# An encoder trunk on one core: its first hundred microseconds reordered, one upper tile pool, embeddings' low parts by DMA

## The chip, the cores and the metric

The kernel runs on one core of a Trainium2 chip. The metric is device time in microseconds of one execution on that core; lower is better. "Before" is the kernel as it stood, "after" is the kernel with the change.

## The reference, cut to what matters

Two layers over 512 positions of width 1024. The change touches mostly the beginning of layer 0: RMSNorm, one input projection whose columns give q, k, v and u, and a bidirectional state-space layer (S5) that works on u.

```python
def rms_norm(x, g):
    y = xf * lax.rsqrt(jnp.mean(xf * xf, axis=-1, keepdims=True) + EPS)
    return y * g

def na_s5_mixer(h, w_in, rpb, ...):
    z = h @ w_in                       # 512x1024 @ 1024x2048
    q, k, v, u = jnp.split(z, 4, axis=-1)
    a_out = neighbourhood_attention(q, k, v, rpb)       # 8 heads x 64
    b_out = s5_glu(s5_bidirectional(u, ...), w_glu, b_glu)   # 32 groups x 16, state 64
    return jnp.concatenate([a_out, b_out], axis=-1) @ w_out

def reference(x, p, ...):
    for i in range(DEPTH):             # 2
        h = rms_norm(x, ...)
        x = x + (na_s5_mixer if i % 2 == 0 else retention_mixer)(h, ...)
        x = x + conv_ffn(rms_norm(x, ffn_norm[i]), ...)     # width 2816, centred conv over 3 positions
        gate = jax.nn.sigmoid(rms_norm(x, ple_norm[i]) @ ple_w_gate[i])
        x = x + gate * (p[i] @ ple_w_proj[i])               # p[i]: 512x256 embeddings
    return rms_norm(x, final_norm)
```

## The kernel before, in words

**Products.** Everything is held transposed: a tile `t` has 128 features on its partitions and 512 positions along it, so the activation x is eight such tiles. Each float32 operand is split in two parts of reduced width, high (a rounded copy, type fp32r) and low (the rest), and a product of one 128-wide block of outputs with eight input tiles is 24 matmuls of 128x512: for each k the low weight with the high x (`L141`), high with high (`L142`), high with low x (`L143`). `proj` makes one such product into one PSUM tile `ps`.

**Weights.** The weights come in 241 chunks of 128x1024; for the first layers a chunk is one product. SyncE's queue (SP) loads them in order into three raw buffers `wr`; a chunk is split three chunks ahead of its product. The high part `wh` is a ScalarE copy (`L113`). The low part `wl` is a VectorE subtract (`L121`, `L123`), but for the chunks in the range `WL_DMA` (6 to 15) ScalarE writes the negated rounded chunk and a GpSimd DMA adds the chunk from memory to it (`L118`, `L119`).

**Beginning of layer 0.** Scale by the norm's weights and split x (`L177` on ScalarE for the high part, `L178` on VectorE for the low one), squares of x for the mean (`L209`), and `prep_small`, a list of small operations on 32-wide tiles for S5 (powers of lambda), of which `do(n)` issues the next n. Then four products for u (`up`); `Rstd` sums the squares over partitions by matmuls with ones (`L241`) and makes 1/rms on VectorE and GpSimd (`v`, `r`); the first product for q (`q0`); `spread` turns 1/rms into a row (`L252`, copied to SBUF by ScalarE in `L255`). `u_out` multiplies u by that row on VectorE, stores it to a scratch in DRAM (`L566`) and loads it back rearranged as `U` (`L567`). `prep_w1` builds S5's input matrices on VectorE (products of `p1r`, `p1i` with 128x512 tiles, line 168), `trans_w1` transposes them (8 matmuls, `L487`, copied by ScalarE in `L489`), and `states` multiplies them with U (`L591`), after every second product. Then follow the other q products, k and v, attention with the S5 recurrence beside it, and the rest of the layer.

**Order of the work.** In this first region the order of ScalarE and VectorE is that in which the code issues (`manual_schedule`); behind it a scheduler places instructions. Each engine executes its instructions strictly in order, and so does SP with the DMAs it issues.

**Tiles.** `T()` takes a 128x512 tile of a pool of 53 buffers (`NT`). With `special=True` it takes one of an extra pool that each feed-forward (20 buffers) and the retention layer (16) opens and closes.

```python
        w_split(3)
        do(99)
        up.append(proj(xg))
        prep_b()
        up.append(proj(xg))
        prep_w1(0, "r")
        up.append(proj(xg))
        prep_w1(0, "i")
        up.append(proj(xg))
        st_ = Rstd(ss, D)
        q0 = proj(xg)
        st_.spread()
        rr, rc = st_.row, st_.col
        for m in range(4):
            u_out(m)
```

Of the kernel before, what the change touches and what calls it, by code (L numbers as in the profile page):

```python
# [53 lines left out]
DO_X = (0, 0, 0, 6, 6, 6, 6, 6)  # L54
# [3 lines left out]
WL_DMA = (6, 16)  # L58
# [3 lines left out]
def trunk_kernel(ctx, tc, xn, xp, pT, wts, vec, s5bc, ddiag, bias, cs, dst, ident, out):  # L62
# [12 lines left out]
    extra = [None]  # L75

    def T(dt=F32, shape=(128, 512), special=False):
        seq[0] += 1
        if special and extra[0] is not None:
            return extra[0].tile(list(shape), dt, name=f"e{seq[0]}", tag="e")  # L80
        return tp.tile(list(shape), dt, name=f"t{seq[0]}", tag="t")
# [63 lines left out]
    def proj(xs):  # L145
        ps = PS()
        for k, x in enumerate(xs):
            mm3(ps, weights(), x, k == 0, k == len(xs) - 1)
        return ps
# [20 lines left out]
    def split(src, scale=None, low=None, special=False):  # L170
        h, l = T(F32R, special=special), T(F32R, special=special)
# [61 lines left out]
    class Rstd:  # L233


        def __init__(self, ss, n):
            ps = PS()
            parts = ss.parts()
# [10 lines left out]
        def spread(self):  # L249
            pr = PS()  # L250
            for j in range(4):
                pe.transpose(out=pr[:, 128 * j:128 * j + 128], in_=self.col[:, j:j + 1].to_broadcast([128, 128]),  # L252
                             identity=idn)
            self.row = T()
            act.activation(out=self.row, in_=pr, func=ACTF.Copy)  # L255
# [4 lines left out]
    class Next:  # L260
# [25 lines left out]
    def mixer0():  # L286
# [15 lines left out]
        svec = sp.tile([128, 96], F32, name="svec")  # L302
        nc.sync.dma_start(out=svec, in_=vec[:, V_LRE:V_LRE + 96])
# [51 lines left out]
        def prep_small():  # L355
# [39 lines left out]
            for have in (1, 2, 4):  # L395
# [11 lines left out]
                q(tt, dve, pwi[:, 1 + have:1 + have + n, :], x, y, ALU.add)  # L407
            lo, hi = slice(0, 64), slice(64, 128)
            for src, a, b in ((pwr, p1r, p2r), (pwi, p1i, p2i)):
                av = a.rearrange("p g j -> p j g")  # L410
                q(act.activation, out=av[lo], in_=src[lo, 7::-1, :], func=ACTF.Copy)
                q(act.activation, out=av[hi], in_=src[hi, 0:8, :], func=ACTF.Copy)
            q(dve.tensor_copy, MA[:, 0, :], pwr[:, 8, :])
# [19 lines left out]
        def prep_blk():  # L433
# [5 lines left out]
            for name in ("r", "i"):  # L439
                for half in range(2):  # L440
                    t = T()
                    v = t.rearrange("p (g d h) -> p g d h", d=2, h=16)
                    pool.memset(t, 0.0)
# [91 lines left out]
        ss = SumSq(dve)  # L535
# [20 lines left out]
        for k in range(KD - SQ_LAG, KD):  # L556
            ss.add(xt[k], sq=True)
# [23 lines left out]
        rr, rc = st_.row, st_.col  # L581
        for m in range(4):
            u_out(m)
        ts(cim, cim, -1.0)
# [91 lines left out]
        for n in range(8):  # L676
            if n < 7:
                prep_w1(n + 1, "r")
                prep_w1(n + 1, "i")
            if n == 2:  # L680
                prep_blk()
            ps = proj(xg) if n else q0
# [7 lines left out]
            if n:  # L690
                after_trans(n - 1)
            next_w2(W2_K[n])
        after_trans(7)
# [4 lines left out]
        def fk_load(i):  # L698
            fk[i] = [T(), T()]
            for k in range(2):  # L700
                nc.sync.dma_start(out=fk[i][k], in_=pT[i, k])

# [9 lines left out]
        for kp in range(4):  # L712
# [10 lines left out]
            if kp == 3:  # L723
                fk[0] = [split(t) for t in fk[0]]
# [107 lines left out]
        def fill(count):  # L832

            for _ in range(min(count, len(fills))):
                i, n = fills.pop(0)
                if i == 0 and n == 4:
                    fk[1] = [split(t) for t in fk[1]]
# [133 lines left out]
        ph.close()  # L971
        nx = Next("ffn0", fast=(1, 3, 5, 6, 7))
        for n in range(KD):
            ps = proj(mix5)
            x = T()
# [5 lines left out]
    def ffn(i, cur, key):  # L981
        ph = ExitStack()
        sp = ph.enter_context(tc.tile_pool(name=f"ff{i}", bufs=1))
        extra[0] = ph.enter_context(tc.tile_pool(name=f"fe{i}", bufs=20))
# [5 lines left out]
        for m in range(KF):  # L990
# [10 lines left out]
            for half in range(2):  # L1001
# [4 lines left out]
                c = T()  # L1006
# [9 lines left out]
            use = m < 10  # L1016
            h, l = T(F32R, special=use), T(F32R, special=use)
# [5 lines left out]
        for n in range(KD):  # L1023
            ps = proj(hid)
            x = T()
# [3 lines left out]
        extra[0] = None  # L1029
# [4 lines left out]
    def ple(i, cur, key):  # L1034
        ph = ExitStack()
        nx = Next(key)
        if key == "fin":
            nx.full = ph.enter_context(tc.tile_pool(name="fin", bufs=1)).tile([128, KD, 512], F32, name="full")
# [15 lines left out]
        def finish(n):  # L1054
            t = sig.pop(n)
            tt(pool if n < PLE_POOL else dve, t, t, prj[n], ALU.mult)
            x = T()
# [26 lines left out]
    def last_out(cur, prj, row, nx, before):  # L1084
# [10 lines left out]
        xl, sq = nx.full[:, KD - 1], T()  # L1095
# [64 lines left out]
    def retention(cur, key):  # L1160
# [3 lines left out]
        extra[0] = ph.enter_context(tc.tile_pool(name="rte", bufs=16))  # L1164
# [15 lines left out]
        def gated(h, sg, ss):  # L1180
# [6 lines left out]
            def two():  # L1187
                hs[0].spread()
                for e in range(4):
                    tt(dve, sg[e], sg[e], hs[0].row, ALU.mult)  # L1190
                    ys[4 * h + e] = split(sg[e], low=pool, special=4 * h + e < 7)
# [66 lines left out]
        extra[0] = None  # L1258
        ph.close()
        nx = Next(key)  # L1260
        for n in range(KD):
# [5 lines left out]
            x = T()  # L1267
# [122 lines left out]
```

## Time and profile before

| | |
|---|---|
| time, median of 3 runs | 1525.79 us (1525.31 to 1527.48) |
| the profiled execution | 1527.03 us, of which 1525.2 us are the span |
| mean granted TensorE clock | 0.991 of full speed |
| TensorE matmul busy | 1495.3 us, 98% of the span |
| VectorE, ScalarE, GpSimd busy | 60%, 40%, 24% |
| share of the chain that ended last | TensorE 84%, VectorE 7% |

The span is the part of the execution that the profile covers; 1.8 us of the profiled execution lie outside it. Busy shares are over the whole span, so a stage with another limit is seen only when the span is cut in stretches. In the rows below PE is TensorE's matmuls, PEld its weight loads, DVE VectorE, ACT ScalarE, POOL GpSimd, SP SyncE.

### The profile page before, as it was taken

To read this page: it belongs to the slowest core of one execution; us is meant where nothing else is said; L and a number is where in the kernel's file an instruction comes from. 1 tells how busy PE (TensorE), PEld (TensorE's weight loads), DVE (VectorE), ACT (ScalarE), POOL (GpSimd) and SP (SyncE) were. 2 spreads that over 40 slices of the span, in tenths; PEclk is the share of its full clock that TensorE was granted. 3 is DMA by queue.
4 is the path that set the end of the run, shared out by engine and by line. 5 is a ranking of instruction groups with operands and counts; after the bars stand their busy time and mean duration, and the time that the engine had idled before them with its cause. 6 is when DMAs were issued, how large, how long until landed. Compare 5 with 4: busy or idle time off the path is not lost.

```text
span 1525.2 us, 18170 instructions
## 1 busy us (share of the span) xinstructions
PE 1495.3 (98%) x7152; PEld 1234.6 (81%) x7152; DVE 915.7 (60%) x1225; ACT 615.1 (40%) x859; POOL 363.9 (24%) x256
## 2 busy tenths in 40 slices
PE   7899999999999999999999999999999999999998
PEld 5687788888888888887888888888888888888887
DVE  8778966877676523485454544534467676743346
ACT  6344755544444322343434232422244444432233
POOL 0100001233232212063141231413122222212105
PEclk9799999999999999999999999999999999999999
DMA  5854392333333433333222222213333333333331
GB/s 198 219 111 141 102 255 61 94 107 97 98 96 98 120 93 93 120 126 108 72 70 84 68 84 69 83 56 97 97 97 97 97 97 97 97 97 96 97 125 56
DMA packets 58934, 158.95 MB, mean 104 GB/s; under 512 B 11744, under 2 KB 15968, under 8 KB 58848
## 3 DMA queue, kind: packets, MB, share of 16 engines
q1 hardware_dynamic: 57408, 152.55, 32.9%
q0 software_dynamic: 1440, 5.24, 2.1%
q8 instruction: 56, 0.92, 0.2%
q14 instruction: 30, 0.25, 0.1%
HBM read 149.94 MB, written 7.83 MB: 103 GB/s over the span
## 4 chain that ended last, share of the span: by engine, by line
PE 84%; DVE 7%; issue 6%; DMA 1%; POOL 1%; ACT 1%; SPq 0%; DVEq 0%; POOLq 0%; ACTq 0%
PE ps L141 27%; PE ps L143 27%; PE ps L142 27%; DVE t L168 4%; PE ps L591 1%; PE ps L926 1%; DMA t<-in_xp_dram 1%; DVE wl L123 1%; DVE t L277 1%; DVE t L774 0%; PE ps L816 0%; PE ps L241 0%; PE ps L487 0%; POOL t L175 0%; DMA vecs<-in_vec_dram 0%
## 5 line engine op out<-in xcount | busy, mean ns | idle before, releaser
L141 PE MATMUL ps<-t,wl 128*128 128x512 f32 x1568 | 615.9, 393 | 11.3 <-DVE wl L551 6.8
L142 PE MATMUL ps<-t,wh 128*128 128x512 f32 x1568 | 611.8, 390 | 0.0
L143 PE MATMUL ps<-t,wh 128*128 128x512 f32 x1568 | 608.8, 390 | 0.7 <-DVE t L277 0.7
L113 ACT ACTIVATE wh<-wr 128x1024 fp32r<-128x1024 f32 x241 | 254.4, 1059 | 556.2 <-PE ps L143 277.5
L123 DVE TENSOR_TENSOR wl<-wr,wh 128x1024 fp32r<-128x1024 f32 x228 | 298.2, 1309 | 288.9 <-ACT wh L113 288.8
L141 PEld LDWEIGHTS ps<-t,wl 128*128 128x128 f32 x1568 | 296.2, 189 | 75.5 <-DVE wl L551 6.8
L143 PEld LDWEIGHTS ps<-t,wh 128*128 128x128 f32 x1568 | 295.8, 189 | 64.2 <-DVE t L277 1.8
L142 PEld LDWEIGHTS ps<-t,wh 128*128 128x128 f32 x1568 | 296.3, 189 | 60.2
L168 POOL TENSOR_TENSOR t<-t,t 128x512 f32<-128x512 f32 x117 | 177.9, 1522 | 457.6 <-ACT t L1014 279.3
L168 DVE TENSOR_TENSOR t<-ps,t 128x512 f32<-128x512 f32 (+1 forms) x86 | 59.3, 698 | 114.8 <-PE ps L143 103.4
L168 DVE TENSOR_TENSOR t<-t,t 128x512 f32<-128x512 f32 (+2 forms) x113 | 96.8, 878 | 27.8 <-ACT t L200 20.7
L168 DVE TENSOR_TENSOR pad<-ps,t 128x512 f32<-128x512 f32 x88 | 60.5, 692 | 82.4 <-PE ps L143 82.4
L1010 DVE SCALAR_TENSOR_TENSOR t<-pad,vecs,t 128x512 f32<-128x512 f32 x88 | 102.3, 1164 | 1.4
L168 POOL TENSOR_TENSOR t<-t 128x512 f32<-128x512 f32 x33 | 50.3, 1527 | 190.0 <-DVE t L168 190.0
L141 PE MATMUL ps<-e,wl 128*128 128x512 f32 x216 | 85.4, 395 | 0.0
L143 PE MATMUL ps<-e,wh 128*128 128x512 f32 x216 | 85.3, 395 | 0.0
L142 PE MATMUL ps<-e,wh 128*128 128x512 f32 x216 | 85.2, 395 | 0.0
L175 POOL TENSOR_TENSOR t<-t,t 128x512 fp32r<-128x512 f32 x41 | 58.6, 1446 | 60.1 <-ACT t L174 51.5
L1011 DVE SCALAR_TENSOR_TENSOR t<-pad,vecs,t 128x512 f32<-128x512 f32 x88 | 70.0, 796 | 2.9
L1008 ACT ACTIVATE t<-pad,vecs 128x512 f32<-128x512 f32 x88 | 70.2, 802 | 3.4 <-DVE pad L168 3.4
L141 PE MATMUL ps<-wh,t 128*128 128x512 f32 x160 | 62.6, 391 | 0.0
L143 PE MATMUL ps<-wl,t 128*128 128x512 f32 x160 | 62.3, 389 | 0.0
(212 smaller groups left out, 1314.1 us busy)
## 6 DMA issues: line engine op xcount, KB each, us to landing
wr<-in_wts_dram SPq DMA_DIRECT2D x241, 512.0 KB, 3.6
wl<-in_wts_dram POOLq DMA_DIRECT2D x10, 512.0 KB, 7.5
pj_scr<-t SPq DMA_DIRECT2D x16, 256.0 KB, 5.1
t<-pj_scr SPq DMA_DIRECT2D x16, 256.0 KB, 4.1
t<-in_xp_dram SPq DMA_DIRECT2D x8, 256.0 KB, 5.3
t<-in_bias_dram SPq DMA_DIRECT2D x8, 256.0 KB, 4.1
Tm<-k_scr SPq DMA_DIRECT2D x8, 256.0 KB, 6.7
t<-in_xn_dram SPq DMA_DIRECT2D x8, 256.0 KB, 6.6
```

The lines of the kernel that those rows point to most:

```text
L113: act.activation(out=h, in_=raw, func=ACTF.Copy)
L123: late.append(lambda: dve.tensor_tensor(out=l, in0=raw, in1=f(h), op=ALU.subtract))
L141: pe.matmul(out=ps, lhsT=lhs[1], rhs=rhs[0], start=start, stop=False)
L142: pe.matmul(out=ps, lhsT=lhs[0], rhs=rhs[0], start=False, stop=False)
L143: pe.matmul(out=ps, lhsT=lhs[0], rhs=rhs[1], start=False, stop=stop)
L168: eng.tensor_tensor(out=out, in0=a, in1=b, op=op)
L175: low.tensor_tensor(out=l, in0=src, in1=f(h), op=ALU.subtract)
L277: self.late.append(lambda: dve.scalar_tensor_tensor(out=l, in0=x, scalar=g, in1=f(h), op0=ALU.mult, op1=ALU.subtract))
L591: pe.matmul(out=pw[:, i, :], lhsT=w1t["ri"[c], g // 4][:, 128 * (g % 4):128 * (g % 4) + 128], rhs=U[:, g, :], start=True, stop=True)
L1008: act.activation(out=c, in_=t[:, 1:513], func=ACTF.Identity, scale=vcol(cw + 44 + j), bias=vcol(V_CB + 44 * i + j))
L1010: dve.scalar_tensor_tensor(out=c, in0=t[:, 0:512], scalar=vcol(cw + j), in1=c, op0=ALU.mult, op1=ALU.add)
L1011: dve.scalar_tensor_tensor(out=c, in0=t[:, 2:514], scalar=vcol(cw + 88 + j), in1=c, op0=ALU.mult, op1=ALU.add)
```

## The change

- The two small loads `svec` and `nvec` are issued by ScalarE's queue ahead of the rest, no longer by SP.
- Beginning: 14 matmuls of a tile of ones with itself (`WARM`), which nothing reads. 12 of S5's small operations go ahead of x's first split and two (the sines, which load another activation table) ahead of the second. All eight splits of x come first, then the second weight chunk, then the rest. The first chunk's three matmuls for each k go high·high, high·low x, low weight·high. The squares are eight ScalarE squares added up by VectorE in one tile after the splits.
- `Rstd` stands after the fourth product as before, but its VectorE part ahead of the S5 input matrices of group 0; the spread stands behind the fifth product as before. Matrices for groups 0 and 1 are made ahead; a group's transposes come one product later, so that two q products (`ready`) stand ahead of them. Four `memset` of GpSimd (in `prep_blk`) become ScalarE copies of ones scaled by zero.
- `WL_DMA` begins at chunk 7, so chunk 6's low part is a VectorE subtract.
- The embeddings p (`fk`, two tiles in each layer) are split by two ScalarE operations and an accumulating GpSimd DMA (`fk_split`), no longer by a VectorE subtract.
- One pool `upper` of 20 buffers lives from the end of the mixer of layer 0 to the end and takes x, the 1/rms row, the convolution's tile `c` and the low parts of the last seven of the 22 feed-forward tiles. The extra pools go, and the last norm's tile `full` becomes eight ordinary tiles.

```diff
-DO_X = (0, 0, 0, 6, 6, 6, 6, 6)
+DO_X = (12, 2, 0, 0, 0, 0, 0, 0)
+WARM = 14
+UPPER = 20
-WL_DMA = (6, 16)
+WL_DMA = (7, 16)
...
-    def mm3(ps, lhs, rhs, start, stop):
+    def mm3(ps, lhs, rhs, start, stop, first=False):
+        if first:
+            pe.matmul(out=ps, lhsT=lhs[0], rhs=rhs[0], start=start, stop=False)
+            pe.matmul(out=ps, lhsT=lhs[0], rhs=rhs[1], start=False, stop=False)
+            pe.matmul(out=ps, lhsT=lhs[1], rhs=rhs[0], start=False, stop=stop)
+            return
...
+        svec = sp.tile([128, 96], F32, name="svec")
+        nc.scalar.dma_start(out=svec, in_=vec[:, V_LRE:V_LRE + 96])
+        nc.scalar.dma_start(out=nvec, in_=vec[:, 0:KD])
...
+        wm = PS()
+        for _ in range(WARM):
+            pe.matmul(out=wm[:, 0:128], lhsT=ones, rhs=ones, start=True, stop=True)
         prep_small()
         for k in range(KD):
+            do(DO_X[k])
             xg.append(split(xt[k], scale=nvec[:, k:k + 1]))
-            do(DO_X[k])
...
-            if k == W1_AT:
-                w_split(1)
-            if k >= SQ_LAG:
-                ss.add(xt[k - SQ_LAG], sq=True)
...
+        w_split(1)
+        do(17)
+        w_split(2)
...
+        for k in range(4):
+            square(k)
...
         w_split(3)
+        for k in range(4, KD):
+            square(k)
         do(99)
         up.append(proj(xg))
+        up.append(proj(xg))
+        while late:
+            late.pop(0)()
+        prep_p1()
         prep_b()
-        up.append(proj(xg))
+        prep_m()
+        do(99)
+        for _ in range(2):
+            up.append(proj(xg))
+        st_ = Rstd(squares, D)
+        ready = [proj(xg)]
         prep_w1(0, "r")
-        up.append(proj(xg))
         prep_w1(0, "i")
-        up.append(proj(xg))
-        st_ = Rstd(ss, D)
-        q0 = proj(xg)
         st_.spread()
+        ready.append(proj(xg))
         rr, rc = st_.row, st_.col
         for m in range(4):
             u_out(m)
+        prep_w1(1, "r")
+        prep_w1(1, "i")
...
         for n in range(8):
-            if n < 7:
-                prep_w1(n + 1, "r")
-                prep_w1(n + 1, "i")
+            if n < 6:
+                prep_w1(n + 2, "r")
+                prep_w1(n + 2, "i")
...
-            ps = proj(xg) if n else q0
+            ps = ready.pop(0) if ready else proj(xg)
...
-            if n:
-                after_trans(n - 1)
+            if n > 1:
+                after_trans(n - 2)
             next_w2(W2_K[n])
+        after_trans(6)
         after_trans(7)
...
+        def fk_split(i):
+            for k in range(2):
+                h_, l_ = T(F32R), T(F32R)
+                act.activation(out=h_, in_=fk[i][k], func=ACTF.Copy)
+                act.activation(out=l_, in_=fk[i][k], func=ACTF.Copy, scale=-1.0)
+                pool.dma_start(out=l_, in_=pT[i, k], accum_op=ALU.add)
...
+        upper[0] = ctx.enter_context(tc.tile_pool(name="upper", bufs=UPPER))
...
-                c = T()
+                c = T(special=True)
...
-            use = m < 10
-            h, l = T(F32R, special=use), T(F32R, special=use)
+            h, l = T(F32R), T(F32R, special=m >= KF - 7)
```

Where the order of the instructions changes. First ScalarE at the very beginning; `t` are x's high parts (from raw tiles and `nvec`), `wh` the first two weight chunks' high parts, `sm_` the small S5 tiles. Before:

```order
L177 ACTIVATE t_151<-t_89,nvec 128x512
L550 ACTIVATE wh_139<-wr_97 128x512
L177 ACTIVATE t_157<-t_90,nvec 128x512
L550 ACTIVATE wh_139<-wr_97 128x512
L209 ACTIVATE t_163<-t_89 128x512
L177 ACTIVATE t_165<-t_91,nvec 128x512
L209 ACTIVATE t_169<-t_90 128x512
L177 ACTIVATE t_172<-t_92,nvec 128x512
L348 ACTIVATE sm_dt<-svec 128x32
```

and now:

```order
L187 ACTIVATE t_178<-t_92,nvec 128x512
L567 ACTIVATE wh_139<-wr_100 128x512
L358 ACT_TABLE_LOAD
L358 ACTIVATE sm_ang<-sm_ang 128x32
L358 ACTIVATE sm_kk<-sm_kk 128x32
L187 ACTIVATE t_186<-t_93,nvec 128x512
L567 ACTIVATE wh_139<-wr_100 128x512
L187 ACTIVATE t_192<-t_94,nvec 128x512
L187 ACTIVATE t_196<-t_95,nvec 128x512
```

The squares have left the space between the splits, and the table load for the sines stands behind the first split instead of the fifth.

Second VectorE around 1/rms (`v`, `r`); `t<-p1r,t` and `t<-p1i,t` are the S5 input matrices, `t<-ps,t` is `u_out`. Before:

```order
L168 TENSOR_TENSOR t_388<-t_388,t_389 128x512
L123 TENSOR_TENSOR wl_359<-wr_252,wh_358 128x1024
L245 TENSOR_SCALAR v_432<-ps_426 128x4
L168 TENSOR_TENSOR v_432<-v_432,r_431 128x4 x2
L230 TENSOR_SCALAR v_432<-v_432 128x4
L168 TENSOR_TENSOR r_431<-r_431,v_432 128x4
L168 TENSOR_TENSOR t_478<-ps_287,t_476 128x512
```

and now:

```order
L125 TENSOR_TENSOR wl_370<-wr_245,wh_369 128x1024
L255 TENSOR_SCALAR v_435<-ps_429 128x4
L240 TENSOR_SCALAR v_435<-v_435 128x4
L178 TENSOR_TENSOR r_434<-r_434,v_435 128x4
L125 TENSOR_TENSOR wl_400<-wr_262,wh_399 128x1024
L178 TENSOR_TENSOR t_475<-p1r,t_350 128x512
L178 TENSOR_TENSOR t_476<-p1i,t_355 128x512
L178 TENSOR_TENSOR t_475<-t_475,t_476 128x512
L178 TENSOR_TENSOR t_480<-p1r,t_355 128x512
L178 TENSOR_TENSOR t_481<-p1i,t_350 128x512
L178 TENSOR_TENSOR t_480<-t_480,t_481 128x512
L178 TENSOR_TENSOR t_524<-ps_294,t_490 128x512
```

Group 0's six matrix operations stood ahead of 1/rms and now stand behind it, with chunk 6's low part (`wl_400`) as a subtract between.

Third TensorE around the first S5 states. Before, the last matmul of the seventh product, group 1's transposes, and `states`:

```order
L143 MATMUL ps_596<-t_233,wh_394 128x512
L487 MATMUL ps_630<-idn,t_496 128x128 x4
L487 MATMUL ps_637<-idn,t_501 128x128 x4
L591 MATMUL ps_644<-U,t_557 128x64 x4
L591 MATMUL ps_644<-U,t_635 128x64 x4
L591 MATMUL ps_655<-U,t_564 128x64 x4
```

and now, from the last matmul of the seventh product, with the first and the last matmul of the eighth:

```order
L150 MATMUL ps_606<-t_213,wh_399 128x512
L502 MATMUL ps_640<-idn,t_475 128x128 x4
L502 MATMUL ps_647<-idn,t_480 128x128 x4
L148 MATMUL ps_664<-t_178,wl_444 128x512
...
L150 MATMUL ps_664<-t_213,wh_443 128x512
L502 MATMUL ps_698<-idn,t_540 128x128 x4
L502 MATMUL ps_705<-idn,t_545 128x128 x4
```

Group 0's transposes come behind the seventh product and group 1's (with `states` behind them) behind the eighth, one product later than before.

## Rows read from the trace of the kernel before

**Rows 1.** Windows: start and end, length; busy us (instructions) of PE, PEld, DVE, ACT, POOL; clock, DMA share, GB/s.

```profile
0.00:20.80 20.80, 12.28 (x32) 8.19 (x33) 13.95 (x37) 15.99 (x28) 0.20 (x4) 0.92 0.86 308
20.80:36.40 15.60, 15.60 (x74) 12.82 (x72) 14.91 (x47) 7.67 (x10) 0.44 (x1) 1.00 0.23 69
36.40:46.00 9.60, 8.10 (x31) 6.45 (x32) 5.31 (x11) 1.90 (x2) 1.65 (x2) 0.82 0.77 218
60.00:77.00 17.00, 13.03 (x50) 11.42 (x51) 13.82 (x28) 6.14 (x12) 0.86 (x1) 0.50 0.80 198
121.00:200.00 79.00, 75.20 (x625) 59.28 (x624) 73.72 (x180) 48.73 (x125) 0.00 (x0) 1.00 0.48 125
300.00:1525.20 1225.20, 1216.10 (x5424) 1004.26 (x5422) 681.93 (x754) 449.65 (x568) 339.84 (x226) 1.00 0.31 93
```

**Rows 2.** Timeline of PE to 39 us: start, duration, instruction, [idle before <- releaser].

```profile
6.79 0.79 PE L141 MATMUL ps<-t,wl 128*128 128x512 f32 x1 [6.79 <-DVE wl L551]
...
20.87 0.39 PE L141 MATMUL ps<-t,wl 128*128 128x512 f32 x1
...
22.23 0.39 PE L141 MATMUL ps<-t,wl 128*128 128x512 f32 x1
...
38.00 0.50 PE L141 MATMUL ps<-t,wl 128*128 128x512 f32 x1 [1.50 <-DVE wl L123]
```

**Rows 3.** Timeline of ACT to 48 us.

```profile
8.55 0.72 ACT L177 ACTIVATE t<-t,nvec 128x512 fp32r<-128x512 f32 x1 [0.44 <-DMA t<-in_xp_dram]
9.18 0.62 ACT L209 ACTIVATE t<-t 128x512 f32<-128x512 f32 x1
...
12.73 1.04 ACT L113 ACTIVATE wh<-wr 128x1024 fp32r<-128x1024 f32 x1
...
14.92 1.28 ACT L348 ACT_TABLE_LOAD   x1
16.22 0.23 ACT L348 ACTIVATE sm_ang<-sm_ang 128x32 f32<-128x32 f32 x1
...
47.91 0.57 ACT L255 ACTIVATE t<-ps 128x512 f32<-128x512 f32 x1
```

**Rows 4.** Timeline of DVE from 25 to 53 us.

```profile
25.61 0.19 DVE L168 TENSOR_TENSOR sm_ta<-pwr 128x32 f32<-128x32 f32 x1
...
30.11 0.26 DVE L348 COPY MA<-pwr 128x32 f32<-128x32 f32 x2
...
36.73 1.22 DVE L123 TENSOR_TENSOR wl<-wr,wh 128x1024 fp32r<-128x1024 f32 x1
...
40.93 0.15 DVE L245 TENSOR_SCALAR v<-ps 128x4 f32<-128x4 f32 x1
...
42.83 0.17 DVE L168 TENSOR_TENSOR r<-r,v 128x4 f32<-128x4 f32 x1
48.51 4.06 DVE L168 TENSOR_TENSOR t<-ps,t 128x512 f32<-128x512 f32 x4 [5.52 <-ACT t L255]
```

**Rows 5.** Timeline of PE from 61 to 81 us.

```profile
61.95 1.11 PE L487 MATMUL ps<-idn,t 128*128 128x128 f32 x4 [4.33 <-DVE t L168]
64.95 1.12 PE L487 MATMUL ps<-idn,t 128*128 128x128 f32 x4 [1.90 <-DVE t L168]
66.20 7.06 PE L591 MATMUL ps<-U,t 128*128 128x64 f32 x32
...
80.42 1.04 PE L487 MATMUL ps<-idn,t 128*128 128x128 f32 x8
```

**Rows 6.** Timeline of SP and its queue: the scratch of u.

```profile
49.62 3.29 SPq L566 DMA_DIRECT2D u_scr<-t  x4
61.90 4.22 SPq L567 DMA_DIRECT2D U<-u_scr  x4
```

**Rows 7.** The page's costliest groups, two of the feed-forward's: count | busy, mean ns | idle before.

```profile
L1010 DVE SCALAR_TENSOR_TENSOR t<-pad,vecs,t 128x512 f32<-128x512 f32 x88 | 102.3, 1164 | 1.4
L1008 ACT ACTIVATE t<-pad,vecs 128x512 f32<-128x512 f32 x88 | 70.2, 802 | 3.4 <-DVE pad L168 3.4
```

More of the change, by code (lines that the diff above doesn't have):

```diff
@@ L74, in trunk_kernel @@
     seq = [0]
-    extra = [None]
+    upper = [None]
     def T(dt=F32, shape=(128, 512), special=False):
         seq[0] += 1
-        if special and extra[0] is not None:
-            return extra[0].tile(list(shape), dt, name=f"e{seq[0]}", tag="e")
+        if special and upper[0] is not None:
+            return upper[0].tile(list(shape), dt, name=f"e{seq[0]}", tag="e")
         return tp.tile(list(shape), dt, name=f"t{seq[0]}", tag="t")
@@ L143, in mm3, with proj @@
         pe.matmul(out=ps, lhsT=lhs[0], rhs=rhs[1], start=False, stop=stop)
-    def proj(xs):
+    def proj(xs, between=None, at=0):
         ps = PS()
         for k, x in enumerate(xs):
-            mm3(ps, weights(), x, k == 0, k == len(xs) - 1)
+            if between and k == at:
+                between()
+            w = weights()
+            mm3(ps, w, x, k == 0, k == len(xs) - 1, first=st["cur"] == 0)
         return ps
@@ L237, in __init__ @@
             ps = PS()
-            parts = ss.parts()
+            parts = ss if isinstance(ss, list) else ss.parts()
             for j in range(4):
@@ L442, in prep_blk @@
                     v = t.rearrange("p (g d h) -> p g d h", d=2, h=16)
-                    pool.memset(t, 0.0)
+                    act.activation(out=t.rearrange("p (a b) -> p a b", b=128),
+                                   in_=ones.rearrange("p (a b) -> p a b", a=1).to_broadcast([128, 4, 128]),
+                                   func=ACTF.Copy, scale=0.0)
                     src = v16(bb[name])
@@ L551, in mixer0, with square @@
                 dve.tensor_tensor(out=l[:, p], in0=raw[:, p], in1=f(h[:, p]), op=ALU.subtract)
-            if k == W1_AT:
-                w_split(1)
-            if k >= SQ_LAG:
-                ss.add(xt[k - SQ_LAG], sq=True)
-        for k in range(KD - SQ_LAG, KD):
-            ss.add(xt[k], sq=True)
+        w_split(1)
+        do(17)
+        w_split(2)
+        squares = []
+        def square(k):
+            t = T()
+            act.activation(out=t, in_=xt[k], func=ACTF.Square)
+            if squares:
+                tt(dve, squares[0], squares[0], t, ALU.add)
+            else:
+                squares.append(t)
+        for k in range(4):
+            square(k)
         up = []
@@ L835, in fill @@
                 i, n = fills.pop(0)
-                if i == 0 and n == 4:
-                    fk[1] = [split(t) for t in fk[1]]
+                if i == 0 and n == 2:
+                    fk_split(1)
                 ps = proj(fk[i])
@@ L1028, in ffn @@
         hid.clear()
-        extra[0] = None
         ph.close()
@@ L1037, in ple @@
         if key == "fin":
-            nx.full = ph.enter_context(tc.tile_pool(name="fin", bufs=1)).tile([128, KD, 512], F32, name="full")
+            nx.full = [T() for _ in range(KD)]
         prj = []
@@ L1190, in two @@
                     tt(dve, sg[e], sg[e], hs[0].row, ALU.mult)
-                    ys[4 * h + e] = split(sg[e], low=pool, special=4 * h + e < 7)
+                    ys[4 * h + e] = split(sg[e], low=pool, special=4 * h + e < 0)
             return one, two
```

34 lines of the change are left out of this document (15 added, 19 removed).

## The prediction

> **What bounds the kernel now.** I read the busy table first: TensorE matmuls fill 98% of the span, so only the other 2% and the stretches at a low clock can be won. The windows then say where these lie. From 300 us to the end the engine is busy 1216.1 of 1225.2 us at full clock [rows 1]: 9.1 us in four fifths of the kernel. The beginning is another matter. The price of work at full clock comes from the timeline: from 20.87 to 22.23 us six matmuls of 128x512, 0.227 us each, so 5.45 us a product of 24; at clock 0.50 twice that [rows 2]. By this price the 32 matmuls up to 20.8 us are 7.3 us of work: 13.5 lost, 6.8 of them ahead of the first matmul. From 36.4 to 46 us 1.5 idle and 8.10 busy at 0.82, another 1.5: 3.0 lost. From 60 to 77 us 4.0 idle and 13.03 at 0.50: 10.5 lost, with 2.3 more of the same wait ahead of 60 us (4.33 ended at 61.95) [rows 1, 2, 5]. Some 29 us in all, and the change reorders just this part. What is waited for there: a low part of the first chunk, another low part at 38.00 (VectorE was busy 14.91 of the 15.60 us before), the S5 matrices of group 1 (4.33 and 1.90), and behind these the states, which multiply with U [rows 1, 2, 5].
>
> The 1/rms row explains the 60s: `r` is done on VectorE at 43.0, but ScalarE copies the row at 47.91, behind four operations on weights; VectorE idles 5.52 us until 48.51, and all S5 matrices stand behind `u_out` [rows 3, 4].
>
> **The change, part by part,** as a walk along TensorE, with the times that rows of before give to each piece.
>
> *First product.* The first matmul waited for VectorE's low half, some 0.6 to 0.7 (half of the 1.22 of a whole chunk [rows 4]). High·high goes first now, so it starts at 6.1. ScalarE then has the table load 1.28 and two sines of 0.14 (7.6), x1 at 0.63 from start to start (8.55 to 9.18), the second half of the chunk 0.5 and six splits at 0.63: 12.6; chunk 1's copy 1.04 to 13.6, VectorE's subtract 1.22 to 14.9 [rows 3, 4]. Product 2 starts there if nothing else is late. Two things can be: x7's landing (x2 was there at 8.55; the five others and chunk 1 are 1.8 MB, 6.0 us at the 308 GB/s of that stretch, so 14.5 at the latest and product 2 at 17.2 [rows 1, 3]), or the clock (21 matmuls at 0.454 from 8.3: 17.8). I take 15.7, near the lower end, since ScalarE waited only 0.44 for x2 although squares and small work gave later tiles more time [rows 3]. The two small loads leave SP, which brings the other loads forward by two issues at most, inside these bounds. The warm-up matmuls run while TensorE waits anyway; what they do to the clock lies within 14.9 to 17.8, and if they ran into the first product they would cost their own time, 14 small matmuls.
>
> One rule speaks against the new place of the table load. In rows 3 it takes 14.92 to 16.20 and the next operation starts at 16.22, so it costs 1.28. The Trainium skill, "ScalarE: Activation LUTs", section "What ACT_TABLE_LOAD costs", counts a drain of 1380 ns to it, 2.66 us a switch. By that, an estimate, x1 to x7 would be 1.4 later and the result below 1.4 us higher, 1516.1; the trace doesn't agree, no gap stands there, and the sum goes by the row.
>
> *Products 2 to 4.* 15.7 + 3 x 5.45 = 32.05, sums of squares 0.9: 32.9, where before they ended at 36.5 (38.00 less 1.50) [rows 2]. Lead 3.6, bounds 1.5 to 4.4. VectorE's work up to chunk 4's low part, from 14.9: 17 small operations 2.5 at 0.15, three low parts 3.4 (1.22 less the 0.09 by which neighbours overlap, as at 9.18), seven adds 4.2, powers 4.5 (25.61 to 30.11), 29.5; with 1.5 of waiting for ScalarE's squares 31.0, before TensorE asks at 32.9 [rows 4]. So the 1.50 wait and the low clock behind it (3.0) go. Little cover, 1.9: if it is gone, they come back.
>
> *1/rms.* The S5 input products (six of 0.6 and four copies, 4.3), 0.4 of small copies and chunk 5's low part 1.1 come ahead of it: 36.8; `v` to `r` took 40.93 to 43.0, so 38.9. Product 5 ends at 38.35, so the spread waits 0.6 and takes 0.4: 39.4. Behind the waiting spread stands product 6, nothing else. Bounds: no wait, or 2 us. ScalarE's copy has no weights ahead of it now. VectorE meanwhile does chunk 6's low part (1.1, new, since that chunk no longer goes by DMA) and six matrices of group 0 (3.9), so `u_out` starts at 44.0 and not 48.51, in place of the 5.52 idle [rows 4].
>
> *To the first states.* Products 6 and 7 to 50.3, group 0's eight transposes 0.9 (1.04 in the row at 80.42, the end overlapped), product 8 to 56.6. VectorE: four `u_out` at 1.0 to 48.0, three operations, then fifteen of 0.6 (which the order puts ahead) and the last sum of group 1: 59.6. Group 1's second transposes thus wait some 2.5 us, against 4.33 and 1.90 before, and end at 60.1 [rows 4, 5]. What is late next is U: from the first store's issue to the states it took 49.62 to 66.20, 16.6 us; 45.1 + 16.6 = 61.7 [rows 5, 6]. Bounds: 60.9, where the transposes' copies allow it (0.8 behind them, as 65.4 to 66.20), and 66.2, no earlier than before. I take 61.7, the same trip, as SP has the same four stores and loads among the same weights. States at full clock take half of 7.06: 65.2. Before, this point (eight products, two groups of transposes, two states) was reached at 80.42 [rows 5]. Lead 15.2.
>
> *Clock.* After 4.33 and 1.90 idle it was 0.50, the 1.2 GHz level, for all of 60 to 77; after 1.50, 0.82 in a window of 9.6 [rows 1]. With 2.5 and 1.6 idle I expect the states at half clock, 3.5 us back; bounds nothing, and 3.5 + 2.0 (nine more matmuls).
>
> *Behind.* Transposes 6 and 7 now follow each other after the last product, so their copies are no longer hidden: twice the 0.8, 1.6 back (0 to 3). The embeddings' four subtracts leave VectorE where it is busy 73.72 of 79 us, 2.4 us; TensorE idles 3.8 there [rows 1]. I take 1.0 won (0 to 2.4). Their two new transfers for each layer go on GpSimd's queue, which is idle there (0.00 busy), and ScalarE, 48.73 of 79 busy, has room for the two operations each.
>
> *Nothing:* the pool `upper`, the tiles of the last norm, ScalarE's copies in place of `memset`. The cover: in a feed-forward two tiles `c` are taken for each two products, 10.9 us, and with x, the row and seven low parts as few as 4 buffers are left, good for two such steps; the work on two tiles is some 2 x (0.80 + 2 x 1.16), 6.2 us [rows 7], and without that cover each of 44 steps would wait for the rest. I price it at nothing, bounds 4 us lost and, from the 9.1 idle, 2 won.
>
> Sum: 15.2 - 3.5 - 1.6 + 1.0 = 11.1 us. The profiled execution, 1525.2 of span and 1.8 around it, would go from 1527.0 to 1515.9; it lies 1.2 above the median of the runs shown, so the median goes from 1525.8 to 1514.7.
>
> **Rivals.** Faster or slower means more than 0.2%, 3.05 us, about what a measurement of this kernel tells from no change.
>
> A, the whole lead is kept: no low clock behind the short waits and U at 60.9. For it: after 1.50 idle only part of the stretch was slow. 15.2 + 0.8 - 1.6 + 1.0 = 15.4, 1510.4 (1508 to 1512).
>
> B, U comes no earlier than before, at 66.2, because its stores and loads share the DMA engines with the same accumulating weight transfers (share 0.80 in 60 to 77 [rows 1]). States at half clock to 73.3, nine slow matmuls 2.0: 75.3, lead 5.1, less 1.6, plus 1.0: 4.5, 1521.3 (1519 to 1522.7).
>
> C, VectorE sets the time from `u_out` to attention's end. Its own lead is 4.5, and the late transposes take 1.6: 2.9, 1522.9, within 0.2%. Against it: it idles 3.2 us even in 60 to 77, where it is waited for, and 543 of the last 1225 [rows 1].
>
> D, slower: U's trip grows. SP executes in order, and the fourth store and the loads stand behind weight loads that wait for raw buffers. The states then end at U + 7.1 with 2.0 of slow matmuls; with the 0.6 behind, no gain is left when U comes at 70.7, a trip of 25.6 in place of 16.6. With twice the trip, 33.2, U is there at 78.3: 7.6 lost, 1533.
>
> **How the numbers follow.** My forecast 0.53 (its own range 1512 to 1518.5), A 0.20, B 0.17, C 0.06, D 0.04. A, B and the forecast are faster: 0.90; C the same: 0.06; D slower: 0.04. The range reaches to A and B with the unknown of the feed-forward: 1507.5 to 1521.5; it leaves out C, D and the outer parts of A and B, under 2 in 10.
>
> **What would show it.** In the changed kernel's profile: the first matmul near 6 us, product 2 near 15.7, no wait at the fifth product, VectorE's first `u_out` near 44 and the idle ahead of it gone; the wait at group 1's transposes near 2.5; the first states near 62, and the clock in the 8 us behind. Behind 200 us all should be as before, shifted by some 11 us. I am wrong if product 2 starts behind 18, if the states come behind 66, if the clock stays at half through two products, or if the feed-forward's blocks wait for tiles `c`.

## The result, and the profile after

The kernel after takes 1507.32 us (median of 4 runs, 1506.71 to 1507.82) against 1526.63 (4 runs, 1525.31 to 1528.38) for before: ratio 0.9873, 95% interval 0.9856 to 0.989. That is 19.3 us less. The forecast was 11.1 us less, 1514.7, and its range ended at 1507.5, just above the measured time. The profiled execution has a span of 1505.9 us against 1525.2, so the trace holds the whole difference.

The windows of the kernel after, cut where the work of [rows 1] now lies (columns as there):

```profile
0.00:17.00 17.00, 14.46 (x58) 11.16 (x59) 11.32 (x34) 13.57 (x23) 0.20 (x4) 1.00 0.91 321
17.00:33.00 16.00, 16.00 (x76) 13.41 (x75) 14.96 (x41) 8.74 (x13) 0.00 (x0) 1.00 0.46 139
33.00:41.00 8.00, 7.54 (x35) 5.94 (x35) 6.66 (x17) 3.45 (x5) 2.01 (x2) 1.00 0.50 163
57.00:65.00 8.00, 4.26 (x24) 3.82 (x22) 7.92 (x18) 3.84 (x8) 0.86 (x1) 0.77 1.13 263
65.00:77.00 12.00, 12.00 (x60) 10.23 (x60) 11.94 (x22) 5.71 (x12) 0.86 (x1) 0.87 0.29 85
```

The stretch at clock 0.50 of [rows 1] has shrunk to 0.77 and 0.87 in 20 us, the one at 0.82 is gone, and VectorE is busy nearly all the time from 38 to 77 us (38.55 of 38.90), where it had idled. The timeline of TensorE after, beside [rows 2, 5]:

```profile
1.06 6.07 PE L560 MATMUL ps<-ones 128*128 128x128 f32 x28 [1.06 <-DVE ones L328]
6.89 0.47 PE L144 MATMUL ps<-t,wh 128*128 128x512 f32 x1
...
15.54 0.50 PE L148 MATMUL ps<-t,wl 128*128 128x512 f32 x1 [0.64 <-DVE wl L123]
...
39.00 0.65 PE L262 MATMUL ps<-idn,r 128*128 128x128 f32 x4 [0.46 <-DVE r L178]
...
59.55 0.66 PE L502 MATMUL ps<-idn,t 128*128 128x128 f32 x4 [2.20 <-DVE t L178]
61.75 3.65 PE L627 MATMUL ps<-U,t 128*128 128x64 f32 x16 [1.54 <-DMA U<-u_scr]
65.16 0.77 PE L148 MATMUL ps<-t,wl 128*128 128x512 f32 x1
65.73 0.63 PE L149 MATMUL ps<-t,wh 128*128 128x512 f32 x1
66.16 0.63 PE L150 MATMUL ps<-t,wh 128*128 128x512 f32 x1
...
68.23 0.39 PE L149 MATMUL ps<-t,wh 128*128 128x512 f32 x1
...
70.98 1.89 PE L627 MATMUL ps<-U,t 128*128 128x64 f32 x16
...
73.94 1.04 PE L502 MATMUL ps<-idn,t 128*128 128x128 f32 x8
```

and of VectorE, beside [rows 4]:

```profile
38.78 0.16 DVE L178 TENSOR_TENSOR r<-r,v 128x4 f32<-128x4 f32 x1
...
43.86 4.08 DVE L178 TENSOR_TENSOR t<-ps,t 128x512 f32<-128x512 f32 x4
...
58.81 0.68 DVE L178 TENSOR_TENSOR t<-t,t 128x512 f32<-128x512 f32 x1
```

Up to the first states the walk of the prediction is met to a few tenths, but for the first matmul: it came at 6.89 instead of 6.1, as the warm-up matmuls ran up to then. Where the rest of the 19.3 comes from is read from instructions that both kernels have: the start in before less the start in after is the lead at that place. In before, the first matmul of attention, the first of the block behind it (`Tm`), and 1/rms of three later norms:

```profile
142.95 1.57 PE L761 MATMUL ps<-t,t 64*128 64x256 f32 x12
...
220.55 0.44 PE L926 MATMUL ps<-Tm,U 128*64 128x128 f32 x4
...
646.18 1.93 POOL L168 TENSOR_TENSOR r<-v,mhalf 128x4 f32<-128x4 f32 x1 [39.35 <-DVE v L245]
...
1115.84 1.93 POOL L168 TENSOR_TENSOR r<-v,mhalf 128x4 f32<-128x4 f32 x1 [30.35 <-DVE v L245]
...
1477.95 1.93 POOL L168 TENSOR_TENSOR r<-v,mhalf 128x4 f32<-128x4 f32 x1 [39.36 <-DVE v L245]
```

and in after:

```profile
130.01 1.57 PE L806 MATMUL ps<-t,t 64*128 64x256 f32 x12
...
206.62 0.44 PE L971 MATMUL ps<-Tm,U 128*64 128x128 f32 x4
...
630.59 1.93 POOL L178 TENSOR_TENSOR r<-v,mhalf 128x4 f32<-128x4 f32 x1 [39.02 <-DVE v L255]
...
1098.52 1.93 POOL L178 TENSOR_TENSOR r<-v,mhalf 128x4 f32<-128x4 f32 x1 [30.00 <-DVE v L255]
...
1458.99 1.93 POOL L178 TENSOR_TENSOR r<-v,mhalf 128x4 f32<-128x4 f32 x1 [39.01 <-DVE v L255]
```

The lead is 12.9 at attention, 13.9 behind it, 15.6 at 646 us of before, 17.3 at 1116, 19.0 at 1478 and 19.3 at the end. So 5.4 us come where the prediction priced everything at nothing. In between, during the 22 blocks of each feed-forward, the lead stays the same; it grows during the products that follow them, and during the retention's output product. TensorE waits for nothing there in either kernel. The page of before had the trace of it, in a view that I read for waits only; groups of TensorE from 500 to 640 us, by form, in before:

```profile
L141 PE MATMUL ps<-t,wl 128*128 128x512 f32 x124 | 48.3, 389 | 0.0
...
L143 PE MATMUL ps<-e,wh 128*128 128x512 f32 x80 | 31.6, 395 | 0.0
```

Matmuls that stream a tile `e` of an extra pool last 395 ns, others 389. From start to start it shows better: in before the 30 matmuls of one run over `e` tiles begin at 527.10, the next over a `t` tile at 534.09, 233 ns each, where `t` tiles have 227:

```profile
527.10 0.40 PE L141 MATMUL ps<-e,wl 128*128 128x512 f32 x1
...
534.09 0.39 PE L141 MATMUL ps<-t,wl 128*128 128x512 f32 x1
```

648 such matmuls (3 x 216) at 6.4 ns are 4.1 us of the 5.4.

### The profile page after: what moved, and what is told of

It reads as the page before. It is cut to its first block, busy times and chain, and to the rows that moved or that the text cites. A ratio compares the mean times of both kernels' runs of the same rounds, so it can differ in the third digit from the quotient of the medians.

```text
span 1505.9 us, 18279 instructions
## 1 busy us (share of the span) xinstructions
PE 1487.4 (99%) x7180; PEld 1234.9 (82%) x7180; DVE 910.3 (60%) x1222; ACT 617.3 (41%) x866; POOL 363.4 (24%) x255
## 4 chain that ended last, share of the span: by engine, by line
PE 86%; DVE 5%; issue 5%; DMA 2%; ACT 1%; POOL 1%; DVEq 0%; SPq 0%; POOLq 0%; ACTq 0%
PE ps L148 27%; PE ps L149 27%; PE ps L150 27%; DVE t L178 2%; PE ps L627 1%; DVE wl L125 1%; PE ps L971 1%; DVE e L178 1%; DMA u_scr<-t 1%; DMA U<-u_scr 1%; PE ps L861 0%; DMA t<-in_xp_dram 0%; PE ps L251 0%; PE ps L502 0%; PE ps L1158 0%
## 5 line engine op out<-in xcount | busy, mean ns | idle before, releaser
L148 PE MATMUL ps<-t,wl 128*128 128x512 f32 (+1 forms) x1776 | 693.7, 391 | 1.8 <-ACT t L885 1.0
L149 PE MATMUL ps<-t,wh 128*128 128x512 f32 (+1 forms) x1776 | 689.9, 389 | 0.0
L150 PE MATMUL ps<-t,wh 128*128 128x512 f32 x1664 | 644.6, 389 | 0.9 <-DVE t L287 0.9
L149 PEld LDWEIGHTS ps<-t,wh 128*128 128x128 f32 x1776 | 334.0, 188 | 67.5
L150 PEld LDWEIGHTS ps<-t,wh 128*128 128x128 f32 x1664 | 312.7, 188 | 66.0 <-DVE t L287 1.3
L178 POOL TENSOR_TENSOR e<-e,e 128x512 f32<-128x512 f32 x44 | 58.7, 1334 | 278.9 <-ACT e L1059 278.9
L178 POOL TENSOR_TENSOR t<-t,t 128x512 f32<-128x512 f32 x49 | 77.3, 1582 | 142.8 <-DVE t L178 128.0
L178 DVE TENSOR_TENSOR pad<-ps,e 128x512 f32<-128x512 f32 x88 | 60.6, 692 | 82.8 <-PE ps L150 82.8
L1055 DVE SCALAR_TENSOR_TENSOR e<-pad,vecs,e 128x512 f32<-128x512 f32 x88 | 101.3, 1153 | 2.3
L1056 DVE SCALAR_TENSOR_TENSOR e<-pad,vecs,e 128x512 f32<-128x512 f32 x88 | 70.0, 796 | 2.9
L1053 ACT ACTIVATE e<-pad,vecs 128x512 f32<-128x512 f32 x88 | 70.2, 803 | 3.3 <-DVE pad L178 3.3
L178 POOL TENSOR_TENSOR t<-e,t 128x512 fp32r<-128x512 f32 x30 | 53.7, 1791 | 35.4 <-ACT t L1062 35.4
```

The costliest lines, as they stand in the source:

```text
L178: eng.tensor_tensor(out=out, in0=a, in1=b, op=op)
L1053: act.activation(out=c, in_=t[:, 1:513], func=ACTF.Identity, scale=vcol(cw + 44 + j), bias=vcol(V_CB + 44 * i + j))
L1055: dve.scalar_tensor_tensor(out=c, in0=t[:, 0:512], scalar=vcol(cw + j), in1=c, op0=ALU.mult, op1=ALU.add)
L1056: dve.scalar_tensor_tensor(out=c, in0=t[:, 2:514], scalar=vcol(cw + 88 + j), in1=c, op0=ALU.mult, op1=ALU.add)
```

## The experiments

**Theories.** S: the place at which a streamed tile starts, against the place of the weight tile, sets the pace of a matmul. All ordinary tiles (2048 bytes a partition) and weight tiles (4096) lie one behind the other, so they start at the same place modulo 256 bytes (the trace shows no addresses; the places are worked out from the order and sizes of the pools). In a feed-forward of before four padded tiles of 514 floats, each rounded up to 2080 bytes, lie ahead of the extra pool: 8320 bytes, which is 128 off; in the retention a tile of 32 bytes makes it 32 off. Rival R: how far up in the partition the tile lies. Rival W: waits for buffers.

**Only the start of the extra pools moved.** The kernel before, plus

```diff
         pads = [sp.tile([128, 514], F32, name=f"pad{j}") for j in range(4)]
+        gap = sp.tile([128, 32], F32, name="gap")
...
         lg = sp.tile([128, 8], F32, name="lg")
+        gap = sp.tile([128, 56], F32, name="gap")
```

> The kernel before, with two unused tiles (128 bytes a partition in each feed-forward, 224 in the retention) that only shift the extra pools' start, so that it stands at the same place modulo 256 bytes as the ordinary tiles and the weight tiles. In before 648 matmuls that stream a tile of an extra pool start 233.5 ns apart on the mean, all others 227. Theory S (where a tile starts decides): these come to 227, 4.2 us less in the profile and some 4 to 5 us less in the time, about 1522. Rival R (how far up in the partition the tile lies decides): still 233.5, time as before, within 2 us. Rival W (the late 5.4 us are waits for buffers that the extra pools cause): no change in the pitch, time as before.

Measured 1522.96 us against 1527.88 for before on that chip, ratio 0.9967 (0.995 to 0.9983), 4.9 us. The same run of 30 matmuls in this kernel:

```profile
524.63 0.39 PE L141 MATMUL ps<-e,wl 128*128 128x512 f32 x1
...
531.43 0.39 PE L141 MATMUL ps<-t,wl 128*128 128x512 f32 x1
```

6.80 us, 227 ns each. An unused tile of 128 bytes takes the slow pace away; the tiles lie higher up than before, so R falls, and W with it, since the buffers are the same. From the first `Tm` to the end of the span this kernel takes 1299.4 us, against 1304.6 in before and 1299.2 in after:

```profile
218.29 0.44 PE L926 MATMUL ps<-Tm,U 128*64 128x128 f32 x4
```

Its span is 1517.7. So behind that place the unused tiles alone give as much as the pools of after.

**All streamed tiles moved.** The kernel after, plus

```diff
+    gap = ctx.enter_context(tc.tile_pool(name="gap", bufs=1)).tile([128, 32], F32, name="gap")
     tp = ctx.enter_context(tc.tile_pool(name="act", bufs=NT))
```

> The kernel after, with one unused tile of 128 bytes a partition ahead of the pool of ordinary tiles, so that all tiles that matmuls stream lie 128 bytes off the weight tiles modulo 256 bytes, as the first feed-forward's extra pool did in before. Theory S: nearly all of the 6,072 matmuls of 128x512 go from 227 to some 233 ns, about 40 us more, 1547. Rival R and rival W: no change, 1505 to 1510. A third way, that only a stream from two pools at different places is slow: no change either, since all streamed tiles stay at one place.

Measured 1539.08 us in a single run, some 31 more than after. 300 us of the first feed-forward, in this kernel and then in after:

```profile
300.00:600.00 300.00, 300.00 (x1288) 241.34 (x1287) 175.27 (x182) 114.74 (x143) 73.68 (x49) 1.00 0.32 97
```

```profile
286.00:586.00 300.00, 300.00 (x1326) 248.39 (x1325) 183.40 (x189) 120.31 (x149) 80.35 (x52) 1.00 0.34 101
```

Both are 100% busy at full clock, and one does 38 matmuls fewer: TensorE's busy share of 100% doesn't show this loss. The 40 us that I expected fell short by 8; 1/rms of the first feed-forward comes only 2.0 later (272.14 against 270.13), so the layers ahead of it, with their waits for VectorE, take little part.

**Weights moved as well.** The same gap ahead of `wraw`, so that weight tiles and streamed tiles move together.

> The kernel after with the same unused tile of 128 bytes, but ahead of the weight tiles too, so that weights and streamed tiles move together. If the distance between the two decides: 227 ns and the time of after, 1507. If the place itself decides: 233 ns and 1539, as when the streamed tiles alone moved.

Measured 1507.8 us in a single run, and the same 1326 matmuls in 300 us as after:

```profile
286.00:586.00 300.00, 300.00 (x1326) 248.57 (x1325) 183.07 (x189) 120.11 (x149) 79.68 (x52) 1.00 0.33 100
```

It is the distance between the two operands that counts, not the place.

**Which distances.** The kernel before with gaps of 48, 16 and 16 floats (first feed-forward, retention, second feed-forward), and with 8, 48 and 160.

> The kernel before with unused tiles that set how far the streamed extra tiles start from the weight tiles, modulo 256 bytes: 64 in the first feed-forward (before 128), 96 in the retention (before 32), 192 in the second feed-forward (before 128). Theory S, any offset but 0 is slow: 231 to 235 ns for all three against 227. Rival: a coarser grid decides, so that 64 and 192 are fast (227) and 96 slow.

> As the run with 64, 96 and 192, with 160 in the first feed-forward, 224 in the retention, and in the second feed-forward 0 modulo 256 but 1024 modulo 2048. Theory S with a period of 256: slow, slow, fast (227). Rival, a period of 2048 as the size of a tile: the third is slow as well.

The mean distance of starts in a run over `e` tiles (21 to 30 matmuls):

| distance modulo 256 bytes | 0 | 32 | 64 | 96 | 128 | 160 | 192 | 224 |
|---|---|---|---|---|---|---|---|---|
| ns from start to start | 226.7 | 233.4 | 229.4 | 234.0 | 233.1 | 234.1 | 233.3 | 233.3 |

The last region of the second kernel, 0 modulo 256 but 1024 modulo 2048, has 226.7, so a period of 2048 falls. One of 512 or 1024 falls too: the extra pool of a feed-forward in the first run with gaps starts 8448 bytes, 256 modulo 512, behind the place where `upper` starts in after (by the order of the pools), and both have 227 ns. So 256 is the period. 64 lies between, below the 231 to 235 that I expected; my rival of a coarser grid is half right there and wrong at 192. The times of the two, one run each, were 1526.52 and 1525.12 us.

**The pools alone, and all but the pools.** The kernel before with the pools of after (its `upper`, `special=True` for x, row and `c`, no extra pools, `full` as a list), and the kernel after with the pools of before:

```diff
-        upper[0] = ctx.enter_context(tc.tile_pool(name="upper", bufs=UPPER))
...
+        upper[0] = ph.enter_context(tc.tile_pool(name=f"fe{i}", bufs=20))
...
-            h, l = T(F32R), T(F32R, special=m >= KF - 7)
+            h, l = T(F32R, special=m < 10), T(F32R, special=m < 10)
```

> The kernel before with only the tile pools of after: the pool of 20 from the end of the first mixer, x, row and the convolution's tile in it, low parts of the last seven of 22. The beginning is that of before. By the leads read from the two traces (13.9 us at the first feed-forward, 19.3 at the end) this part is worth 5.4 us: 1526.6 less 5.4 is 1521.2, whatever its mechanism. My prediction's step (the pools are worth nothing) expects 1526.6 within 1.5.

> The kernel after with the pools of before (an extra pool in each feed-forward and the retention, the last norm's tile in a pool of its own): the beginning, the embeddings' split and chunk 6 alone. By the leads 13.9 us faster than before, 1512.7; with the step that the pools are worth nothing it would be the time of after, 1507.3. The 648 matmuls that stream extra tiles are at 233 ns again.

Measured 1523.14 us, ratio to before 0.9967 (0.9956 to 0.9979), 4.7 less; and 1513.4, ratio 0.991 (0.9895 to 0.9924). By ratio that is 0.37% or 5.6 us more than after. These are the two sides of the 5.4; the beginning with the rest of the change is the other 14 us (1527.88 less 1513.4 is 14.5). Which of the edits at the beginning carry the 14 was tested only for those that follow.

**Parts of the beginning.** The kernel after without the 14 matmuls of ones:

```diff
-WARM = 14
+WARM = 0
...
-        wm = PS()
```

> The kernel after without the 14 matmuls of ones at the start. My prediction put the second product between 14.9 and 17.8 us, the upper end if the first product runs at half clock (0.43 us a matmul): if the warm-up is what lifted the clock, the first product's last matmuls are at 0.43, the second product starts near 17.5 instead of 15.54 and the time is about 2 us longer, 1509.3. Rival: the clock rises by itself as the product begins, or product 2 waits for VectorE anyway: within 0.7 of 1507.3.

Measured 1507.66 us (1505.48 to 1510.25), no difference. Its first products:

```profile
6.08 0.79 PE L144 MATMUL ps<-t,wh 128*128 128x512 f32 x1 [6.08 <-ACT wh L566]
...
10.16 0.63 PE L144 MATMUL ps<-t,wh 128*128 128x512 f32 x1
10.58 0.63 PE L145 MATMUL ps<-t,wh 128*128 128x512 f32 x1
...
12.33 0.40 PE L144 MATMUL ps<-t,wh 128*128 128x512 f32 x1
...
15.40 0.50 PE L148 MATMUL ps<-t,wl 128*128 128x512 f32 x1 [0.15 <-DVE wl L123]
```

Matmuls start 0.43 us apart until 11.9 us here, as where the granted clock reads 0.50, and 0.23 behind it, so the warm-up does lift the clock. (The clock column doesn't show this: its first record in this trace begins at 11.85, and it reads 1.00 for 0 to 17 us.) The first matmul starts at 6.08, 0.8 ahead of after's, as no warm-up matmul stands in its way. But product 2 waits for chunk 1's low part in both (0.64 with the warm-up, 0.15 without), and starts at 15.40 instead of 15.54. My expectation let 21 matmuls run slowly, and it was about ten.

Group 0's matrices ahead of 1/rms again:

```diff
+        prep_w1(0, "r")
+        prep_w1(0, "i")
         st_ = Rstd(squares, D)
         ready = [proj(xg)]
-        prep_w1(0, "r")
-        prep_w1(0, "i")
```

> The kernel after with group 0's six matrix operations ahead of 1/rms again. My walk: the spread then waits some 4.3 us in place of 0.5, but u_out starts where it did (both stand ahead of it), product 8 ends at 60.5, group 1's transposes no longer wait, and the states start near 62.0 in place of 61.75; with a stretch at half clock behind the longer wait some 1 to 2 us in all, 1508.3 to 1509.3. Rival, the earlier 1/rms carries the gain by itself: the whole 4 us, 1511.5.

Measured 1507.82 us (1505.93 to 1508.37), ratio to before 0.9868 (0.9854 to 0.9883). The wait that was put back, and the first states:

```profile
42.85 1.11 PE L262 MATMUL ps<-idn,r 128*128 128x128 f32 x4 [4.27 <-DVE r L178]
...
64.21 1.90 PE L627 MATMUL ps<-U,t 128*128 128x64 f32 x16
```

The rival's 1511.5 falls. The 4.27 us of waiting cost nothing, for behind it the 2.20 and the 1.54 are gone and the states run at full clock (1.90 against 3.65). They start 2.2 later than my walk said, as the half clock now comes behind the 4.27, in product 6, yet the next transposes start at 73.30 against 73.94 in after. TensorE's idle time between 15 and 107 us is 4.9 us here and 4.8 in after: it only changed its place.

Transposes one product later still:

```diff
-            if n > 1:
-                after_trans(n - 2)
+            if n > 2:
+                after_trans(n - 3)
...
+        after_trans(5)
         after_trans(6)
```

> The kernel after with the transposes of a group yet one product later (three q products ahead of the first, the last three groups behind the last product). In after TensorE waits 2.2 us for group 1's transposes and 1.5 for U, and works at half clock for some 3 us behind. If these waits are only a matter of when U and the matrices are ready, a product fills them: the states start near 63 without a wait, and 5 to 6 us are won, 1501.5 to 1502.5. Rival, the time moves on: transposes and states together behind the last product give 1 to 2 us back, 1503 to 1504. Rival, VectorE sets the time from there on: within 1 us of 1507.3.

Measured 1504.0 us (1502.16 to 1507.43), ratio to before 0.9846 (0.9826 to 0.9867): the fastest of all, 0.27% or 4.1 us ahead of after by the ratios, whose intervals overlap a little. This is the upper end of the rival by which the time moves on. A product fills the waits but for 1.24 here and 0.60 ahead of the states at 92.61:

```profile
64.60 2.00 PE L627 MATMUL ps<-U,t 128*128 128x64 f32 x16 [1.24 <-ACT t L504]
...
101.51 0.44 PE L531 MATMUL ps<-t,t 128*128 128x128 f32 x2
```

The last row stands at 106.28 in after, so 4.8 us are won by then, but 1/rms of the first feed-forward comes only 2.7 earlier (267.43 against 270.13): attention gives 2.1 back. Part of that is the clock, at half behind a wait of 1.1 there, where after has 1.00 throughout (columns as in [rows 1]):

```profile
157.00:161.00 4.00, 3.88 (x14) 3.20 (x14) 4.00 (x18) 3.75 (x14) 0.00 (x0) 0.57 0.18 66
```

The embeddings' low parts on VectorE again:

```diff
-                act.activation(out=l_, in_=fk[i][k], func=ACTF.Copy, scale=-1.0)
-                pool.dma_start(out=l_, in_=pT[i, k], accum_op=ALU.add)
+                tt(dve, l_, fk[i][k], f(h_), ALU.subtract)
```

> The kernel after with the embeddings' low parts as VectorE subtracts again (at the same places, without the accumulating transfers). My prediction gave their removal 1.0 us (0 to 2.4), and the lead grows by 1.0 in the attention stage (12.9 at its first matmul, 13.9 behind it): 1508.3 if it is this. Rival: the 1.0 comes from the attention's other waits falling differently, within 0.4 of 1507.3.

Measured 1511.37 us, ratio to before 0.9893 (0.9879 to 0.9908), by ratio 0.20% or 3.1 us more than after. From the last place named to the first `Tm`, its longest wait, and the window behind this wait:

```profile
107.15 0.44 PE L531 MATMUL ps<-t,t 128*128 128x128 f32 x2
...
209.75 0.44 PE L970 MATMUL ps<-Tm,U 128*64 128x128 f32 x4
```

```profile
PE ps L830 <- ACT t L848: 2.6, 1, 2.6
```

```profile
162.00:165.50 3.50, 3.39 (x24) 2.22 (x23) 3.40 (x12) 2.85 (x8) 0.00 (x0) 0.51 0.20 75
```

102.6 us, against 100.34 in after (106.28 to 206.62), 2.3 more, which is about the 2.4 us of four subtracts. Not all of it is waiting: ScalarE, for which TensorE waits 2.6, had waited 1.45 and 0.96 for VectorE, and behind this wait the clock is at half for some 3.4 us, which after doesn't have. 0.9 more were lost ahead of it, where U came at 61.80 with a wait of 1.80; that the edit did this isn't shown, and kernels with the same beginning differ as much there.

## Why the prediction was right and wrong

| step | predicted | measured |
|---|---|---|
| first matmul, product 2 | 6.1, 15.7 | 6.89, 15.54 |
| sums of squares done, r done | 32.9, 38.9 | 32.9, 38.9 |
| u_out, wait of group 1's transposes | 44.0, 2.5 | 43.86, 2.20 |
| first states | 61.7 | 61.75 |
| lead behind them, clock taken off | 15.2 - 3.5 = 11.7 | 11.9 |
| "Behind": up to attention | -1.6 | +1.0 |
| embeddings, net of attention | +1.0 | +1.0 |
| "Nothing": pools and the rest | 0 | +5.4 |

The 11.9 is 80.42 [rows 5] less 73.94 - 5.45, since one more product stands ahead of the third transposes now. These leads come from one pair of traces. The first states start between 64.59 and 67.41 in five kernels with the beginning of before, and between 60.89 and 61.80 in six with the order of after (one of them without the warm-up), so the leads up to there are good to some 1.5 us, and that 61.7 was met to a tenth is in part luck. The 14 us of the whole beginning rest on the medians of the runs above.

**The step that failed** is "*Nothing:* the pool `upper`", priced at 0 where 5.4 us were won. It looked for buffers that come free too late and found cover, rightly: in both feed-forwards the lead doesn't move. That the change of pools also changes where streamed tiles start wasn't in it at all. The bound of 2 us won was drawn from the 9.1 us of idle time, and the gain lay in the busy time, where 648 matmuls took 233 ns each. The run with gaps of 128 and 224 bytes shows that as the cause: from the first `Tm` to the end it takes 1299.4, 5.2 less than before, and the kernels with the pool `upper`, but for the one with all streamed tiles moved, take 1299.2 to 1300.5. The count of matmuls gives 4.1 of the 5.2; the other 1.1 lies within the 1.3 by which these kernels differ. With nothing for the pools the time would have been in the range: the kernel after with the pools of before took 1513.4.

**"Behind" had the wrong sign.** It claimed that transposes 6 and 7 now follow each other, and are no longer hidden. They did so in before, with the copy's wait that I charged to the change:

```profile
113.07 1.91 PE L487 MATMUL ps<-idn,t 128*128 128x128 f32 x16
115.58 2.00 PE L591 MATMUL ps<-U,t 128*128 128x64 f32 x16 [0.60 <-ACT t L489]
```

After has 48 records of states in one piece behind them and no wait. I had read the loop's end as new when it was old.

**The `memset`,** also under "Nothing", were not nothing. In before a VectorE operation beside them takes 2.80 us, and it stands ahead of the matrices of group 1, for which TensorE waited 4.33:

```profile
52.48 2.80 DVE L331 TENSOR_SCALAR t<-t 128x512 f32<-128x512 f32 x1
...
52.75 2.25 POOL L443 MEMSET t<- 128x512 f32 x4
```

In after, with ScalarE's copies, it stands behind these matrices and takes 0.42:

```profile
59.41 0.42 DVE L341 TENSOR_SCALAR t<-t 128x512 f32<-128x512 f32 x1
```

So it is in every trace: 1.49, 1.86, 1.92 and 2.80 us where it overlaps the `memset`, 0.44 in the one kernel where it ends ahead of them (64, 96 and 192 bytes), 0.41 to 0.43 in the eight kernels without them. The walk doesn't name this operation, and what its 2.4 us are worth in the time no run shows.

**The clock term** held for another reason than stated. Only 16 of the 32 records of states ran at half clock, 1.8 us; seven matmuls behind them gave 1.4 more: 3.2 in place of 3.5. The price of half clock was also too high: such a matmul starts 0.43 us behind the last (65.73 and 66.16 above), 1.9 times the 0.227, not twice.

**The embeddings** came out at 1.0 net, which must be 2.3 won and about 1.3 of the lead given back in attention: with the subtracts its stretch up to `Tm` takes 78.87 us, against 77.60 in before. That would be rival C's mechanism on a small scale, and the version with transposes one later shows such a loss directly (2.1 of 4.8), a part of it by the clock. Rivals A, B and D did not come: from the first store's issue at 44.96 to the states at 61.75 it is 16.8 us, against 16.6 in before [rows 5, 6].

**The table load's rule.** By the Trainium skill, "ScalarE: Activation LUTs", section "What ACT_TABLE_LOAD costs", x1's split would have come 1.4 us later, an estimate. The load ran from 6.24 for 1.28 us and the next operation began at 7.53; the trace doesn't agree with the drain, as before. (In before the load stood behind the sixth split of x, not the fifth: that split starts at 14.20, the load at 14.92.)

## What to carry to other kernels

Look at the distance from start to start of equal matmuls, not only at waits and busy shares: a group that is a few per cent slower than its twin is a finding, and moving a pool can change it without any edit of the work. Lay streamed tiles and weight tiles so that they start at the same place modulo 256 bytes (shown here for float32r matmuls of 128x512 alone); an odd tile ahead of a pool undoes it for all behind. And before a wait is priced as a gain, follow what stands behind it: 4.3 us put back at the spread cost nothing here, since as much waiting went away behind it.

## What the hardware showed that I had not expected

A float32r matmul of 128x512 at full clock takes 226.7 ns from start to start when the streamed tile and the weight tile start at the same place modulo 256 bytes, and 229.4 to 234.1 at the seven other distances in steps of 32; moving both by 128 bytes changes nothing. Why the chip does this no run here shows. And a VectorE operation of 0.42 us took up to 2.80 beside GpSimd's `memset`.
